# Raw weights of two turns on chip in the first feed-forward product, token sums behind its first turn, and the last operand pair scaled out of place

## The chip, the cores and the metric

The kernel runs on one core of one Trainium2 chip. The metric is the device time of one execution in microseconds, lower is better. Three timed runs of the kernel before give a median of 1869.41 us (1862.83 to 1870.68). The trace shown here is of one profiled execution, which took 1867.55 us.

TensorE multiplies matrices into PSUM banks. VectorE (DVE in the profile), ScalarE (ACT) and GpSimd (POOL) work element by element, and SyncE (SP) issues the DMA transfers. In the program each engine has one fixed order of instructions, so what stands behind a waiting instruction on its engine starts later.

## The reference

One layer of a hybrid decoder over 1024 prompt tokens and 8 sample tokens, in fp32, with a model width of 1024. The change concerns the last two of its steps:

```
x += crossattn(rmsnorm(x), memory K/V)       # 4 heads, 256 memory rows, output product o @ w_xo
x += relu(rmsnorm(x, norm_ffn_g) @ w_up)^2 @ w_down     # 1024 -> 4096 -> 1024
y  = rmsnorm(x, final_g)
rmsnorm(x, g) = x * rsqrt(mean(x * x, -1) + 1e-6) * g
```

## The kernel before

Tokens lie along the free axis (1032 columns, as two halves of HT = 516), features along the partitions. Every fp32 operand of a product is split into a high part (a cast on ACT to fp32r) and a low part (source minus high part, on DVE); `split` (L103 for the cast, L104 for the subtraction) does it, and a product takes three matmuls: high by high, high by low, low by high.

`cross_out` computes the output product of the cross attention, one slice of 128 features at a time (L136), adds the residual x on DVE (L1211), squares the sum on ACT and adds the squares up on POOL into the tile `ssx` (L1217), writes x to DRAM, and scales it in place by `norm_ffn_g` (`scaled`, L1118). The tiles `yq[0..3]` hold two slices each, that is one "pair" of features in four blocks of 516 columns (b11, b12, b21, b22).

The feed-forward part replaces the 8 block products of a 2x2 by 2x2 block product by 7 (a Strassen scheme). `features` builds the seven token-side combinations of each pair by subtraction and splits them into the operands `c_cb0`, `c_cb1` (pairs 0 and 1) and `c_o0`, `c_o1` (pairs 2 and 3). The product then runs in 32 turns: 16 for `w_up` and 16 for `w_down`. In every turn TensorE goes through the 7 steps of `STEPS`: A11, S2, S3, S1, S4, A12, A22, with 24 matmuls of 128x258 each (L1190, tiles `ps_A` and `ps_S`). Four PSUM banks take the products in rotation.

`weights(step, it)` prepares the weights of turn `it` in seven steps: step 0 loads the raw weights, two halves `wr0` (blocks A11 and A21) and `wr1` (A12 and A22), 512 KB each (L1160); steps 1 to 6 form S3, S2, S1 and S4 on POOL (`comb`, L1149) and split each block. `turn` issues, for each step, the matmuls, then `evict`, then `ahead(n)`. `ahead(n)` in turn `it` runs step n of the weights of turn `it+1`, and at n = 6 step 0 of turn `it+2`. All raw weights take their tile from the pool tag `wst`.

In an up turn `up` collects the products in one of the four tiles, `yq[it % 4]`: a copy on ACT for A11 (L1283), additions of PSUM on DVE for the others (L1274), then relu and square on ACT (L1277, L1278). Four results `ht` of further subtractions on POOL (`sub`, L1265) and three blocks of yq go to the DRAM tensor `d_h` (L1261), all issued by SP. From turn 15 on `stage` brings the first combinations of the down turns back from `d_h` into yq tiles (L1380), and the tokens' operands are split from there; later ones come through `fetch` (L1341).

The scale of the norm is applied late: `token_sums` sums the squares per token on TensorE (`ps_ms`, L1242), DVE makes `ms` and its reciprocal (L1248, L1249), and TensorE spreads it over the partitions (`ps_msb`, L1254), from where it is copied over `ssx` (L1256). `residual` multiplies x by it (L1325) and subtracts (L1333) in turns 1 to 12. In the kernel before this stands ahead of the first turn.

Program order is not written out by hand for each engine: a scheduler places the instructions of each engine in the order in which the operands are expected, so a change in the program can also change an engine's order elsewhere.

Of the kernel before, what the change touches and what calls it, by code (L numbers as in the profile page):

```python
# [19 lines left out]
P = 128  # L20
# [3 lines left out]
NB = 8  # L24
# [46 lines left out]
class K:  # L71
# [1036 lines left out]
    def operand(self, pl, tag):  # L1108

        t = pl.tile([P, 2, 7, HT], F32R, tag=tag, name=f"c_{tag}")  # L1110
        return t[:, 0], t[:, 1]

    def scaled(self, i):

        x = self.yq[i]
        for j in range(2):
            xj = x[:, 2 * j:2 * j + 2]
            self.nc.vector.tensor_scalar(xj, xj, self.g["norm_ffn_g"][:, 2 * i + j:2 * i + j + 1], None, op0=ALU.mult)  # L1118

    def features(self, *pairs):  # L1120

        nc = self.nc
        t2 = {i: self.hr.tile([P, HT], F32, tag="hr", name="ft") for i in pairs}
        for c, x, y, z in ((0, 0, None, None), (3, 0, 1, 0), (4, 4, 3, 0), (5, 1, 3, 1), (2, 3, None, None), (1, 2, None, None), (6, 2, 2, 4)):
            for i in pairs:
                blk = [self.yq[i][:, n] for n in range(4)] + [t2[i]]
                if y is not None:
                    (nc.vector if i == 3 and c in (3, 4) else nc.gpsimd).tensor_tensor(blk[x], blk[y], blk[z], op=ALU.subtract)
                if c != 3:
                    self.split(self.b[i][0][:, c], self.b[i][1][:, c], blk[x])  # L1130
            if c == 5:
                for i in pairs:
                    self.split(self.b[i][0][:, 3], self.b[i][1][:, 3], self.yq[i][:, 0])

    def weights(self, step, it):
# [61 lines left out]
    def cross_out(self):  # L1197
        nc, a = self.nc, self.a
        N0 = HALF + NB
        xm = lambda m: self.yq[m // 2][:, 2 * (m % 2):2 * (m % 2) + 2].rearrange("p h t -> p (h t)")  # L1200
        blocks = ((0, N0 // 2), (N0, T), (N0 // 2, N0))
        for ms in ((0, 1), (2,), (3,), (4,), (5,), (6,), (7,)):
# [3 lines left out]
            for m, (b0, b1) in [(m, b) for b in blocks for m in ms]:  # L1206
# [11 lines left out]
            for m in ms:  # L1218
                nc.sync.dma_start(self.d_x[m], xm(m))
            if ms[-1] % 2:  # L1220
                self.scaled(ms[-1] // 2)
            if ms[-1] in (1, 3):
                self.features(ms[-1] // 2)

    def ffn(self, f1):
# [21 lines left out]
        for rr, cc in areas:  # L1247
            nc.vector.tensor_scalar(ms[rr, cc], ps[rr, cc], 1.0 / D, RMS_EPS, op0=ALU.mult, op1=ALU.add)  # L1248
            nc.vector.reciprocal(r2[rr, cc], ms[rr, cc])  # L1249
        for tiles in ((0, 1, 2, 3), (8,), (4, 5, 6, 7)):  # L1250
            ps = bank("ps_msb")[:, 0]
            for j, i in enumerate(tiles):
                n = P if i < 8 else NB
                nc.tensor.matmul(ps[:, j * P:j * P + n], ms[0:n, i:i + 1].broadcast_to([n, P]), self.ident[0:n, 0:n], start=True, stop=True)  # L1254
            c0, n = TC[tiles[0]].start, P * len(tiles) if tiles[0] < 8 else NB
            nc.vector.tensor_copy(self.ssacc[:, c0:c0 + n], ps[:, 0:n])  # L1256
        msb = self.ssacc.rearrange("p (h t) -> p h t", h=2)
# [52 lines left out]
        def down(n, ps):  # L1310
            y = yq[it % 4]
            op = ALU.subtract if n in ("S4", "A22") else ALU.add
# [23 lines left out]
        def sums(j):  # L1336
            nc.sync.dma_start(yq[j].rearrange("p (m h) t -> p m (h t)", m=2), self.d_x[2 * j:2 * j + 2].rearrange("k p t -> p k t"))

# [275 lines left out]
```

## Time and profile before

| | us |
|---|---|
| median of three runs | 1869.41 (1862.83 to 1870.68) |
| profiled execution | 1867.55 |
| span in its trace | 1865.8 |
| TensorE busy | 1677.5 (90%) |
| DVE busy | 1251.6 (67%) |
| POOL busy | 842.5 (45%) |
| ACT busy | 763.1 (41%) |

The span is what the trace covers; the execution is 1.75 us longer. Busy time is summed over the whole span. A stretch of the span is read by its own busy times, and by the granted clock of TensorE beside them, where 1.00 is the higher of its two levels (2.4 GHz) and 0.50 the lower one (1.2 GHz). Feed-forward turns are told apart by the start of their first `ps_S` product, S2, which follows A11.

### The profile page before, as it was taken

How to read it: one execution, taken by the hardware profiler on the slowest of the kernel's cores; microseconds unless marked ns; L12 is line 12 of the kernel's file. 1: busy time of each engine (PE TensorE's matmuls, PEld its weight loads, DVE VectorE, ACT ScalarE, POOL GpSimd, SP SyncE). 2: the span in 40 equal slices, each digit the busy share in tenths (PEclk: the TensorE clock that was granted, in tenths of full speed). 3: DMA queues.
4: the chain of work that ended last, by engine and by line, in shares of the span. 5: the costliest groups of instructions: out<-in, count | busy, mean ns of one | idle time of the engine just before them, and what ended most of it. 6: DMA issues, size and time to landing. Idle time of an engine off the chain costs nothing. (4 is left out here: it accounts for less than half of the span.)

```text
span 1865.8 us, 36912 instructions
## 1 busy us (share of the span) xinstructions
PE 1677.5 (90%) x14667; PEld 1550.3 (83%) x14667; DVE 1251.6 (67%) x2316; ACT 763.1 (41%) x1453; POOL 842.5 (45%) x648
## 2 busy tenths in 40 slices
PE   6988888998995699999999988889998889999997
PEld 5887777887884688878887888889998889999997
DVE  5797687679768855656555456445554498888795
ACT  4535443554532244423332333333333364444442
POOL 6541342134247664654333566674544453322242
PEclk8999777999996899999999998999999999999998
DMA  4313312211223574664443423664444586554542
GB/s 136 112 57 95 111 57 81 66 50 54 68 68 91 147 235 119 213 189 137 149 146 125 148 91 113 185 197 125 126 126 125 171 290 211 153 153 139 148 126 103
DMA packets 248541, 244.20 MB, mean 131 GB/s; under 512 B 24936, under 2 KB 191232, under 8 KB 248368
## 3 DMA queue, kind: packets, MB, share of 16 engines
q1 hardware_dynamic: 248324, 241.82, 42.4%
q8 instruction: 116, 1.90, 0.4%
q14 instruction: 57, 0.47, 0.1%
q10 hardware_dynamic: 44, 0.01, 0.0%
HBM read 179.95 MB, written 61.83 MB: 130 GB/s over the span
## 5 line engine op out<-in xcount | busy, mean ns | idle before, releaser
L1190 PE MATMUL ps_S<-c_cb,wS 128*128 128x258 f32 x1536 | 227.5, 283 | 7.0 <-DVE yq L1315 5.3
L1190 PE MATMUL ps_S<-c_o,wS 128*128 128x258 f32 x1536 | 227.0, 283 | 0.0
L136 PE MATMUL ps_g<-xh,wh 128*128 128x256 f32 (+1 forms) x704 | 216.7, 308 | 11.1 <-DVE raw L369 6.2
L104 POOL TENSOR_TENSOR wl<-wst,wh 128x1024 fp32r<-128x1024 f32 x70 | 169.7, 2424 | 113.1 <-ACT wh L103 99.4
L136 PE MATMUL ps_g<-xl,wh 128*128 128x256 f32 (+1 forms) x704 | 212.2, 302 | 0.8 <-DVE xl L104 0.8
L136 PE MATMUL ps_g<-xh,wl 128*128 128x256 f32 (+1 forms) x704 | 210.7, 299 | 0.1
L1190 PE MATMUL ps_A<-c_cb,wA 128*128 128x258 f32 x1152 | 179.1, 292 | 34.7 <-DVE yq L1274 34.7
L1190 PEld LDWEIGHTS ps_S<-c_cb,wS 128*128 128x128 f32 x1536 | 203.3, 190 | 7.5 <-issue 5.4
L104 DVE TENSOR_TENSOR wS<-rS,wS 128x512 fp32r<-128x512 f32 x96 | 100.4, 1046 | 158.9 <-ACT wS L103 158.9
L1190 PEld LDWEIGHTS ps_S<-c_o,wS 128*128 128x128 f32 x1536 | 202.4, 190 | 0.0
L1190 PEld LDWEIGHTS ps_A<-c_cb,wA 128*128 128x128 f32 x1152 | 158.7, 197 | 37.4 <-issue 36.0
L136 PE MATMUL ps_g<-o,wh 128*128 128x260 f32 (+1 forms) x768 | 176.2, 324 | 7.1 <-DVE yq L1211 3.6
L1190 PE MATMUL ps_A<-c_o,wA 128*128 128x258 f32 x1152 | 177.7, 291 | 0.2 <-DVE c_o L104 0.2
L1149 POOL TENSOR_TENSOR rS<-wr,rS 128x512 f32<-128x512 f32 x64 | 90.6, 1416 | 172.1 <-DMA wr<-in_w_down_dram 82.7
L1190 PEld LDWEIGHTS ps_A<-c_o,wA 128*128 128x128 f32 x1152 | 159.0, 198 | 0.4 <-DVE c_o L104 0.4
L136 PEld LDWEIGHTS ps_g<-xh,wh 128*128 128x128 f32 x704 | 142.8, 203 | 17.1 <-DVE raw L369 6.7
L103 ACT CAST wh<-wst 128x1024 fp32r<-128x1024 f32 x92 | 96.1, 1046 | 135.8 <-PE ps_g L136 67.4
L136 PEld LDWEIGHTS ps_g<-xl,wh 128*128 128x128 f32 x704 | 142.4, 202 | 5.8 <-issue 2.0
L103 ACT CAST wS<-rS 128x512 fp32r<-128x512 f32 x96 | 57.8, 617 | 217.2 <-POOL rS L1149 209.1
L136 PEld LDWEIGHTS ps_g<-o,wh 128*128 128x128 f32 x768 | 128.6, 191 | 20.2 <-issue 6.0
L136 PEld LDWEIGHTS ps_g<-xh,wl 128*128 128x128 f32 x704 | 141.7, 201 | 3.7 <-issue 1.4
L136 PE MATMUL ps_g<-o,wl 128*128 128x260 f32 (+1 forms) x384 | 124.6, 325 | 3.1 <-POOL wl L104 3.1
(481 smaller groups left out, 3891.6 us busy)
## 6 DMA issues: line engine op xcount, KB each, us to landing
hb<-d_h SPq DMA_DIRECT2D x105, 258.0 KB
wst<-in_w_in_dram SPq DMA_DIRECT2D x44, 512.0 KB
d_h<-ht SPq DMA_DIRECT2D x64, 258.0 KB
wr<-in_w_up_dram SPq DMA_DIRECT2D x32, 512.0 KB
wr<-in_w_down_dram SPq DMA_DIRECT2D x26, 512.0 KB
d_h<-yq SPq DMA_DIRECT2D x48, 258.0 KB
wst<-in_w_out_dram SPq DMA_DIRECT2D x16, 512.0 KB
ck<-in_cache_mem_k_dram SPq DMA_DIRECT2D x32, 256.0 KB
```

What stands on the lines that cost most here:

```text
L103: (heng or nc.scalar.copy)(hi, src)
L104: (eng or nc.vector).tensor_tensor(lo, src, hi.bitcast(F32), op=ALU.subtract)
L136: nc.tensor.matmul(ps, l[:, k, :], r[:, cols], start=(k == 0 and i == 0), stop=(k == kt - 1 and i == 2))
L1149: nc.gpsimd.tensor_tensor(R[n], R[x], R[y], op=op)
L1190: nc.tensor.matmul(ps[:, s], l[:, i, :], r[:, c, cols], start=k == 0 and j == 0, stop=k == 3 and j == 2)
```

## The change

The edits, in the order of the program:

- In `cross_out` raw x lies in the yq tiles 2, 3, 0, 1 instead of 0, 1, 2, 3. Pair 3, raw in `yq[1]`, is scaled out of place into `yq[3]`, block of columns by block (a new `tensor_scalar` on DVE), instead of in place in two instructions.
- The token-side subtractions are put into `first_diff` and `second_diffs`, called as soon as a pair is scaled; `features` then mostly splits. The order of the splits is 0, 4, 5, 3, 2, 1, 6.
- The token sums and their spreading (`mean_squares`) move from before turn 0 into `ahead(6)` of turn 0; `residual` moves by one turn, to turns 2 to 13.
- The raw weights of odd up turns are loaded into `yq[2]`, those of even turns into the `wst` tiles. Step 0 for turn `it+2` is called at n = 0 of turn `it` (for `it` under 15) instead of n = 6.
- The up turns collect their products in two tiles, `yq[(it + 1) % 2]`, instead of four.
- The first three stage loads move: the first to the end of turn 13, the second to the start of turn 15 (before, both were in turn 14); the stage tiles and the tiles of the down turns' sums are numbered anew to fit.

The core of the diff:

```
+    def first_diff(self, i):
+        b11, b12, b21, b22 = self.blocks(i)
+        t1 = self.hr.tile([P, HT], F32, tag="hr", name="t1")
+        self.nc.gpsimd.tensor_tensor(t1, b12, b11, op=ALU.subtract)
+        self.td[i] = [t1]
+
+    def second_diffs(self, i):
+        b11, b12, b21, b22 = self.blocks(i)
+        t2 = self.hr.tile([P, HT], F32, tag="hr", name="t2")
+        eng = self.nc.vector if i == 3 else self.nc.gpsimd
+        eng.tensor_tensor(t2, b22, self.td[i][0], op=ALU.subtract)
+        eng.tensor_tensor(b12, b22, b12, op=ALU.subtract)
+        self.td[i].append(t2)
...
+        for c in (0, 4, 5, 3, 2, 1, 6):
             for i in pairs:
-                blk = [self.yq[i][:, n] for n in range(4)] + [t2[i]]
-                if y is not None:
-                    (nc.vector if i == 3 and c in (3, 4) else nc.gpsimd).tensor_tensor(blk[x], blk[y], blk[z], op=ALU.subtract)
-                if c != 3:
-                    self.split(self.b[i][0][:, c], self.b[i][1][:, c], blk[x])
-            if c == 5:
-                for i in pairs:
-                    self.split(self.b[i][0][:, 3], self.b[i][1][:, 3], self.yq[i][:, 0])
+                b11, b12, b21, b22 = self.blocks(i)
+                t1, t2 = self.td[i]
+                if c == 6:
+                    self.nc.gpsimd.tensor_tensor(b21, b21, t2, op=ALU.subtract)
+                src = {0: b11, 4: t2, 5: b12, 3: t1, 2: b22, 1: b21, 6: b21}[c]
+                self.split(self.b[i][0][:, c], self.b[i][1][:, c], src)
...
-                t = self.wp.tile([P, 4, 256], F32, tag="wst", name=f"wr{r}")
+                if it < 16 and it % 2:
+                    t = self.yq[2].rearrange("p b t -> p (b t)")[:, r * 1024:(r + 1) * 1024].rearrange("p (i m) -> p i m", i=4)
+                else:
+                    t = self.wp.tile([P, 4, 256], F32, tag="wst", name=f"wr{r}")
...
+        raw = [self.yq[i] for i in (2, 3, 0, 1)]
+        self.xs = raw[0:3] + [raw[1]]
+        self.td = {}
+        xm = lambda m: raw[m // 2][:, 2 * (m % 2):2 * (m % 2) + 2].rearrange("p h t -> p (h t)")
...
+                if m >= 6:
+                    xg = self.xs[3][:, 2 * (m - 6):2 * (m - 6) + 2].rearrange("p h t -> p (h t)")[:, b0:b1]
+                    nc.vector.tensor_scalar(xg, x, self.g["norm_ffn_g"][:, m:m + 1], None, op0=ALU.mult)
...
-            if ms[-1] % 2:
-                self.scaled(ms[-1] // 2)
-            if ms[-1] in (1, 3):
-                self.features(ms[-1] // 2)
+            i = ms[-1] // 2
+            if ms[-1] in (1, 3, 5):
+                self.scaled(i)
+                self.first_diff(i)
+                self.second_diffs(i)
+                if i < 2:
+                    self.features(i)
+            elif ms[-1] == 6:
+                self.first_diff(3)
+            elif ms[-1] == 7:
+                self.second_diffs(3)
...
-        ps = token_sums("ps_ms")
...
+        def mean_squares():
+
+            ps = token_sums("ps_ms")
...
-            y = yq[it % 4]
+            y = yq[(it + 1) % 2]
...
-            if n == 6 and it < 30:
+            if (n == 6 or it < 15 and n == 0) and it < 30 and it + 2 not in self.w:
                 self.weights(0, it + 2)
             c = self.STEPS[n][1]
-            if 1 <= it <= 12 and n == 1:
-                residual((it - 1) // 3, (it - 1) % 3)
-            if it == 14 and n in (1, 4):
-                stage(n // 4)
+            if it == 0 and n == 6:
+                mean_squares()
+            if 2 <= it <= 13 and n == 1:
+                residual((it - 2) // 3, (it - 2) % 3)
+            if it == 13 and n == 6:
+                stage(0)
             if it == 15:
+                if n == 0:
+                    stage(1)
                 if n == 2:
                     stage(2)
                 for i, b in enumerate(self.b):
                     self.split(b[0][:, c], b[1][:, c], staged[n][:, i])
-                if n in (0, 1, 2, 4):
-                    stage({0: 3, 1: 4, 2: 5, 4: 6}[n])
+                if n in (0, 1, 3, 4):
...
-            x = yq[(0, 1, 2, 0, 1, 2, 1)[n]]
+            x = yq[(3, 2, 1, 3, 2, 3, 2)[n]]
...
+        acc = [yq[i] for i in (1, 3, 2, 0)]
```

In the rows below a name with a number is one tile instance. On TensorE, at the passage from the last product of the cross attention (`ps_g`, L136) to turn 0, the kernel before has:

```order
L136 MATMUL ps_g_12520<-o0_9361,wh_12457 128x260 x2
L136 MATMUL ps_g_12520<-o0_9361,wl_12458 128x260
L1242 MATMUL ps_ms_12636<-ones_487,ssx_11742 128x1 x8
L1242 MATMUL ps_ms_12636<-ones_487,ssx_11742 8x1
L1254 MATMUL ps_msb_12652<-ident_116,ms_12646 128x128 x4
L1254 MATMUL ps_msb_12658<-ident_116,ms_12646 128x8
L1254 MATMUL ps_msb_12661<-ident_116,ms_12646 128x128 x4
L1190 MATMUL ps_A11_12667<-c_cb0_11747,wA11_12569 128x258 x3
L1190 MATMUL ps_A11_12667<-c_cb1_11748,wA11_12569 128x258 x3
L1190 MATMUL ps_A11_12667<-c_o0_12553,wA11_12569 128x258 x3
```

and the changed kernel (`ps_A11`, `ps_S2` and so on are the products of the steps; its matmuls are L1206):

```order
L136 MATMUL ps_g_12534<-o0_9361,wh_12469 128x260 x2
L136 MATMUL ps_g_12534<-o0_9361,wl_12470 128x260
L1206 MATMUL ps_A11_12644<-c_cb0_11747,wA11_12585 128x258 x3
L1206 MATMUL ps_A11_12644<-c_cb1_11748,wA11_12585 128x258 x3
L1206 MATMUL ps_S2_12674<-c_cb0_11747,wS2_12591 128x258 x3
L1206 MATMUL ps_S2_12674<-c_cb1_11748,wS2_12591 128x258 x3
L1206 MATMUL ps_S3_12708<-c_cb0_11747,wS3_12595 128x258 x3
L1206 MATMUL ps_S3_12708<-c_cb1_11748,wS3_12595 128x258 x3
L1206 MATMUL ps_S1_12737<-c_cb0_11747,wS1_12598 128x258 x3
L1206 MATMUL ps_S1_12737<-c_cb1_11748,wS1_12598 128x258 x3
L1206 MATMUL ps_A11_12644<-c_o0_12569,wA11_12585 128x258
L1206 MATMUL ps_S2_12674<-c_o0_12569,wS2_12591 128x258
```

The sums and their spreading are gone from between the two, and the parts of A11, S2, S3 and S1 that need only `c_cb` stand ahead of the first that need `c_o`. In the changed kernel the sums stand on TensorE between the last step of turn 0 and the first of turn 1:

```order
L1206 MATMUL ps_A22_12843<-c_o0_12569,wA22_12607 128x258 x3
L1206 MATMUL ps_A22_12843<-c_o1_12570,wA22_12607 128x258 x3
L1272 MATMUL ps_ms_12877<-ones_487,ssx_11742 128x1 x8
L1272 MATMUL ps_ms_12877<-ones_487,ssx_11742 8x1
L1286 MATMUL ps_msb_12891<-ident_116,ms_12642 128x128 x4
L1286 MATMUL ps_msb_12897<-ident_116,ms_12642 128x8
L1286 MATMUL ps_msb_12900<-ident_116,ms_12642 128x128 x4
L1206 MATMUL ps_A11_12910<-c_cb0_11747,wA11_12702 128x258 x3
L1206 MATMUL ps_A11_12910<-c_cb1_11748,wA11_12702 128x258 x3
```

They now lie behind the whole of turn 0. On POOL, around the results `ht` of turn 7 (collected in `yq3` before), the kernel before has, with `wr*_14604` the raw weights of turn 9:

```order
L1265 TENSOR_TENSOR ht_14526<-yq3_11746 128x516
L1149 TENSOR_TENSOR rS3_14664<-wr0_14604 128x512
L1265 TENSOR_TENSOR ht_14561<-yq3_11746 128x516
L1265 TENSOR_TENSOR ht_14564<-yq3_11746,ht_14561 128x516
L1265 TENSOR_TENSOR ht_14609<-yq3_11746,ht_14564 128x516
L1149 TENSOR_TENSOR rS2_14669<-wr1_14606,rS3_14664 128x512
L1149 TENSOR_TENSOR wr0_14604<-wr0_14604,wr1_14606 128x4x128
L1149 TENSOR_TENSOR rS2_14669<-wr1_14606,rS2_14669 128x512
```

and the changed kernel (turn 7 collects in `yq0`; `yq2` holds the raw weights of turn 9, `wr*_14627` those of turn 10, and the operation of L1149 is L1162):

```order
L1297 TENSOR_TENSOR ht_14519<-yq0_11743 128x516
L1162 TENSOR_TENSOR rS2_14662<-yq2_11745,rS3_14657 128x512
L1297 TENSOR_TENSOR ht_14554<-yq0_11743 128x516
L1297 TENSOR_TENSOR ht_14557<-yq0_11743,ht_14554 128x516
L1297 TENSOR_TENSOR ht_14598<-yq0_11743,ht_14557 128x516
L1162 TENSOR_TENSOR rS2_14662<-yq2_11745,rS2_14662 128x512
L1162 TENSOR_TENSOR rS3_14901<-wr0_14627 128x512
L1162 TENSOR_TENSOR wr0_14627<-wr0_14627,wr1_14629 128x4x128
```

S2 of turn 9 moved ahead of three of the `ht`, and S3 and S1 of turn 9 are no longer in this stretch; in their place stand S3 and S1 of turn 10. On SP, in the same stretch, the kernel before has:

```order
L1261 DMA d_h_70<-yq3_11746 128x516
L1160 DMA wr0_14604<-in_w_up_dram 128x4x256
L1261 DMA d_h_70<-ht_14526 128x516
L1261 DMA d_h_70<-yq3_11746 128x516
L1261 DMA d_h_70<-ht_14561 128x516
L1261 DMA d_h_70<-yq3_11746 128x516
L1261 DMA d_h_70<-ht_14564 128x516
L1160 DMA wr1_14606<-in_w_up_dram 128x4x256
L1261 DMA d_h_70<-ht_14609 128x516
```

and the changed kernel:

```order
L1176 DMA wr0_14627<-in_w_up_dram 128x4x256
L1293 DMA d_h_70<-ht_14519 128x516
L1293 DMA d_h_70<-yq0_11743 128x516
L1293 DMA d_h_70<-ht_14554 128x516
L1293 DMA d_h_70<-yq0_11743 128x516
L1293 DMA d_h_70<-ht_14557 128x516
L1293 DMA d_h_70<-ht_14598 128x516
L1176 DMA wr1_14629<-in_w_up_dram 128x4x256
L1293 DMA d_h_70<-yq1_11744 128x516
```

The place of the two loads among the stores is much the same; before, they bring the weights of turn 9, now those of turn 10.

## Rows read from the trace of the kernel before

**Rows 1.** The page: busy time, its share of the span, and instructions, by engine.

```profile
PE 1677.5 (90%) x14667; PEld 1550.3 (83%) x14667; DVE 1251.6 (67%) x2316; ACT 763.1 (41%) x1453; POOL 842.5 (45%) x648
```

**Rows 2.** Windows by stage: length, PE, PEld, DVE, ACT, POOL busy, clock, DMA share, GB/s.

```profile
1110.00:1130.00 20.00, 7.62 (x48) 7.01 (x47) 17.78 (x17) 9.68 (x17) 14.57 (x9) 0.69 0.25 79
1157.90:1489.90 332.00, 298.47 (x2355) 295.96 (x2354) 164.13 (x196) 125.19 (x223) 178.86 (x131) 0.95 0.50 153
1489.90:1541.00 51.10, 42.78 (x339) 41.82 (x338) 47.08 (x64) 33.33 (x61) 24.09 (x11) 0.97 0.85 290
1541.00:1561.20 20.20, 20.20 (x171) 20.20 (x170) 20.20 (x26) 8.01 (x13) 11.96 (x8) 1.00 0.62 184
```

**Rows 3.** Critical chain in the down turns: start, us, what.

```profile
1541.14 11.50 PE ps_S L1190 x96
1552.64 8.63 PE ps_A L1190 x72
1561.27 11.48 PE ps_S L1190 x96
```

**Rows 4.** Waits in the up turns, 1160 to 1500: engine and line, releaser, total, times, longest.

```profile
ACT wS L103 <- POOL rS L1149: 146.5, 14, 12.2
...
POOL rS L1149 <- DMA wr<-in_w_up_dram: 85.3, 24, 6.3
...
PE ps_A L1190 <- DVE yq L1274: 33.5, 14, 4.0
```

**Rows 5.** Critical chain around turns 7 to 9.

```profile
1324.12 1.29 POOL ht L1265
...
1333.59 4.92 DMA wr<-in_w_up_dram
1338.58 1.32 POOL rS L1149
...
1340.57 1.11 DVE wS L104
1341.68 0.60 DVE yq L1274
1342.29 1.31 DVE wS L104
1343.60 0.62 DVE yq L1274
...
1351.50 0.49 ACT yq L1283
```

**Rows 6.** Groups of the up turns on DVE, 1160 to 1500, each shape apart.

```profile
L104 DVE TENSOR_TENSOR wS<-rS,wS 128x512 fp32r<-128x512 f32 x42 | 53.5, 1274 | 132.6 <-ACT wS L103 132.6
L1274 DVE TENSOR_TENSOR yq<-ps_S,yq 128x516 f32<-128x516 f32 x71 | 47.4, 683 | 3.8 <-PE ps_S L1190 3.7
```

**Rows 7.** Timeline of 1112 to 1142 on TensorE.

```profile
1120.01 2.84 PE L1242 MATMUL ps_ms<-ones,ssx 128*128 128x1 f32 x14 [4.62 <-POOL ssx L1217]
1130.74 4.36 PE L1254 MATMUL ps_msb<-ident,ms 128*128 128x128 f32 x18 [7.89 <-DVE ms L1248]
1134.86 0.96 PE L1190 MATMUL ps_A<-c_cb,wA 128*128 128x258 f32 x6
```

**Rows 8.** Timeline of the same stretch on DVE.

```profile
1114.24 0.43 DVE L1211 TENSOR_TENSOR yq<-ps_g,yq 128x260 f32<-128x260 f32 x1 [0.77 <-PE ps_g L136]
...
1115.19 0.69 DVE L104 TENSOR_TENSOR wS<-wr,wS 128x512 fp32r<-128x512 f32 x1
...
1122.13 5.12 DVE L104 TENSOR_TENSOR c_o<-yq,c_o 128x516 fp32r<-128x516 f32 x3
```

**Rows 9.** Timeline of 1157 to 1159.5 on TensorE.

```profile
1157.90 0.89 PE L1190 MATMUL ps_S<-c_cb,wS 128*128 128x258 f32 x6
```

**Rows 10.** Critical chain from turn 15 on.

```profile
1498.87 4.50 DMA d_h<-ht
1503.38 8.30 DMA hb<-d_h
```

More of the change, by code (lines that the diff above doesn't have):

```diff
@@ L1111, in operand, with blocks @@
         return t[:, 0], t[:, 1]
+    def blocks(self, i):
+        return [self.xs[i][:, n] for n in range(4)]
     def scaled(self, i):
-        x = self.yq[i]
+        x = self.xs[i]
         for j in range(2):
@@ L1118, in scaled @@
             self.nc.vector.tensor_scalar(xj, xj, self.g["norm_ffn_g"][:, 2 * i + j:2 * i + j + 1], None, op0=ALU.mult)
+    def first_diff(self, i):
[10 more added lines that the diff above has]
+        self.td[i].append(t2)
     def features(self, *pairs):
-        nc = self.nc
-        t2 = {i: self.hr.tile([P, HT], F32, tag="hr", name="ft") for i in pairs}
-        for c, x, y, z in ((0, 0, None, None), (3, 0, 1, 0), (4, 4, 3, 0), (5, 1, 3, 1), (2, 3, None, None), (1, 2, None, None), (6, 2, 2, 4)):
+        for c in (0, 4, 5, 3, 2, 1, 6):
             for i in pairs:
-                blk = [self.yq[i][:, n] for n in range(4)] + [t2[i]]
-                if y is not None:
-                    (nc.vector if i == 3 and c in (3, 4) else nc.gpsimd).tensor_tensor(blk[x], blk[y], blk[z], op=ALU.subtract)
-                if c != 3:
-                    self.split(self.b[i][0][:, c], self.b[i][1][:, c], blk[x])
-            if c == 5:
-                for i in pairs:
-                    self.split(self.b[i][0][:, 3], self.b[i][1][:, 3], self.yq[i][:, 0])
+                b11, b12, b21, b22 = self.blocks(i)
[4 more added lines that the diff above has]
+                self.split(self.b[i][0][:, c], self.b[i][1][:, c], src)
     def weights(self, step, it):
@@ L1199, in cross_out @@
         N0 = HALF + NB
-        xm = lambda m: self.yq[m // 2][:, 2 * (m % 2):2 * (m % 2) + 2].rearrange("p h t -> p (h t)")
+        raw = [self.yq[i] for i in (2, 3, 0, 1)]
+        self.xs = raw[0:3] + [raw[1]]
+        self.td = {}
+        xm = lambda m: raw[m // 2][:, 2 * (m % 2):2 * (m % 2) + 2].rearrange("p h t -> p (h t)")
         blocks = ((0, N0 // 2), (N0, T), (N0 // 2, N0))
@@ L1243, in token_sums @@
             return ps
-        ps = token_sums("ps_ms")
         ms, r2 = f1.tile([P, 9], F32, name="ms"), f1.tile([P, 9], F32, name="r2")
[L1247 to L1256, printed above, removed]
+        def mean_squares():
+            ps = token_sums("ps_ms")
+            for rr, cc in areas:
+                nc.vector.tensor_scalar(ms[rr, cc], ps[rr, cc], 1.0 / D, RMS_EPS, op0=ALU.mult, op1=ALU.add)
+                nc.vector.reciprocal(r2[rr, cc], ms[rr, cc])
+            for tiles in ((0, 1, 2, 3), (8,), (4, 5, 6, 7)):
+                ps = bank("ps_msb")[:, 0]
+                for j, i in enumerate(tiles):
+                    n = P if i < 8 else NB
+                    nc.tensor.matmul(ps[:, j * P:j * P + n], ms[0:n, i:i + 1].broadcast_to([n, P]), self.ident[0:n, 0:n], start=True, stop=True)
+                c0, n = TC[tiles[0]].start, P * len(tiles) if tiles[0] < 8 else NB
+                nc.vector.tensor_copy(self.ssacc[:, c0:c0 + n], ps[:, 0:n])
         msb = self.ssacc.rearrange("p (h t) -> p h t", h=2)
@@ L1310, in down @@
         def down(n, ps):
-            y = yq[it % 4]
+            y = acc[it % 4]
             op = ALU.subtract if n in ("S4", "A22") else ALU.add
@@ L1336, in sums @@
         def sums(j):
-            nc.sync.dma_start(yq[j].rearrange("p (m h) t -> p m (h t)", m=2), self.d_x[2 * j:2 * j + 2].rearrange("k p t -> p k t"))
+            nc.sync.dma_start(acc[j].rearrange("p (m h) t -> p m (h t)", m=2), self.d_x[2 * j:2 * j + 2].rearrange("k p t -> p k t"))
         def fetch(pair, n):
@@ L1358, in ahead @@
                     self.split(b[0][:, c], b[1][:, c], staged[n][:, i])
-                if n in (0, 1, 2, 4):
-                    stage({0: 3, 1: 4, 2: 5, 4: 6}[n])
+                if n in (0, 1, 3, 4):
+                    stage({0: 3, 1: 4, 3: 5, 4: 6}[n])
                 if n == 3:
@@ L1363, in ahead @@
             if t == 1 and n == 0:
-                y = yq[3]
+                y = yq[0]
                 sub(5, y[:, 3], y[:, 1])
@@ L1389, in ffn @@
             if t >= 12:
-                y = yq[t - 12]
+                y = acc[t - 12]
                 for k in (2, 1):
@@ L1416, in ffn @@
         nc.sync.dma_start(gfin, a["final_g"].unsqueeze(0).broadcast_to([P, D]))
-        yt = lambda j, m: yq[j].rearrange("p (m h) t -> p m (h t)", m=2)[:, m]
+        yt = lambda j, m: acc[j].rearrange("p (m h) t -> p m (h t)", m=2)[:, m]
         n = 0
```

## Prediction

> **What bounds the kernel now.** I read the page first, then windows by stage, then the waits and the chain inside the stage that stood out. The page shows TensorE busy for 1677.5 us of the span [rows 1], so 188 us at most are idle, and the question is where. The windows answer that: in a down turn TensorE is busy without a break at a clock of 1.00, while in the up turns it is busy for 298.47 of 332 us at 0.95, at the passage from up to down for 42.78 of 51.1, and ahead of turn 0 for 7.62 of 20 [rows 2]. The change touches just these three stretches.
>
> A turn that nothing holds up lasts 1561.27 - 1541.14 = 20.13 us: 96 matmuls of S in 11.5 and 72 of A in 8.63 [rows 3]. From S2 of turn 1 to S2 of turn 15 are 14 turns in 332.0 us, where 14 x 20.13 = 281.8 would do, so the up turns lose 50.2 us. Of these TensorE waits 33.5 us, once in each turn, for a DVE eviction of PSUM [rows 4]; the other 17 agree with a clock of 0.95 instead of 1.00 over 332 us [rows 2].
>
> DVE was not short of time: it is busy 164.13/14 = 11.7 us per up turn, POOL 12.8 and ACT 8.9 [rows 2]. The chain tells why the eviction is late [rows 5]. The load of the second half of the raw weights of turn 9 goes out at 1333.59, behind the stores of turn 7, and takes 4.92 us. POOL forms S2 at 1338.58, ACT casts it, DVE splits it at 1340.57, and only behind this split stands the next eviction, at 1341.68; then again a split and an eviction. TensorE stands meanwhile, its banks full. The largest waits of the stretch are links of this one chain: POOL for the weights' DMA, 85.3 us, and ACT for POOL, 146.5 us [rows 4].
>
> **The change, part by part.** *Raw weights of two turns on chip.* The order shows the two loads of the stretch at the same places between the stores of turn 7, but they now bring turn 10 and not turn 9. The halves of turn 9 have landed a turn, some 20 us, before S2 is formed, so the 4.92 us of the DMA and its place in SP's queue leave the chain. S2 of turn 9 stands on POOL directly behind the first `ht` of turn 7, which was at 1324.12, and not behind all four; it would be formed near 1325.4 and split some 3 us later, near 1328.4, where before the split ended at 1341.68 [rows 5]. DVE then waits for products of TensorE, which is how it should be. What is late next is S4 of turn 9, which stands behind the last `ht`: that ends near 1334.5 by three of some 1.4 us, S4 is split near 1337.5, and its split's place on DVE is behind the eviction of A12 of turn 8, near 1325.7 + 11.5 + 2.9 = 1340. So some 2.5 us of slack at the tightest place, and the loads of POOL and DVE leave 7 us per turn. S3 and S1 of the turn after come behind and have most of a turn. I take a period of 20.3 us: 14 x 20.3 = 284.2, a gain of 48. Bounds: 50.2, all of it, and 42, 0.6 us left in each turn.
>
> The two output tiles in place of four add a wait: ACT's copy of A11 of turn 9 must find the stores of turn 7 done. In the chain before, that copy is at 1351.50 [rows 5], some 17 us behind the last of these stores; with two stalls less it comes some 7 us sooner. A store takes 4.50 us [rows 10]. Some 5 us remain, and I cost this at nothing; without that cover each us too late is 14 us in all, and ACT's casts of weights queue behind it.
>
> *Sums behind turn 0, features, last pair out of place.* Before, TensorE does 14 of the 18 sums at 1120.01, the spreading at 1130.74 to 1135.1, and A11 only at 1134.86 [rows 7], although the last gemm's eviction is at 1114.24 [rows 8]. Turn 1's S2 begins at 1157.90 [rows 9]. In the new order TensorE begins turn 0 right behind the gemm, with 24 matmuls that need only pairs 0 and 1, and goes on as splits of pairs 2 and 3 come. From 1114.7 DVE has 19 instructions up to the last of these splits. One takes 0.69 us at 1115.19 and 1.71 at 1122.13 [rows 8]: 13 or 32 us. I take 1.2, between the two, since fewer POOL subtractions lie beside: 23 us, the last split at 1137.5, and A22, which needs it, ends 2.9 later. With TensorE at the lower clock for part of that, as it had 0.69 on average in 1110 to 1130 [rows 2], I put turn 0's end at 1142. Now the sums are on the path: 2.84/14 x 18 = 3.65, then 4.36 for the spreading, 8.0 in the slow stretch of before [rows 7], half of it at the full clock; I take 6. DVE stands at `ms` meanwhile with one split of weights behind, which is hidden. Then A11, 8.63/3 = 2.9, and S2 of turn 1 at 1151: 7 us gained. Bounds: with 13 us of DVE TensorE is the limit, from the first split near 1118 with 144 matmuls at 0.12 us, 1135.5, then 4.1 and 2.9: 1142.5, a gain of 15. With 32 us: 1147 + 2.9 + 8.0 + 2.9 = 1161, a loss of 3. The residual one turn later moves nothing in sum, since POOL has room; its two loads and stores per turn go with it on SP.
>
> *The passage.* From S2 of turn 15 to the down turns are 51.1 us in place of 40.3. DVE is busy for 47.08 of them and the DMA engines for 0.85 at 290 GB/s [rows 2]; the splits and loads that make it so all stay. Only one stage load of 1.06 MB comes before turn 15 now, not two. If transfers decide, that costs 1.06 MB / 290 GB/s = 3.6 us; if DVE does, nothing. The chain there runs through a load of 8.30 us [rows 10]. The weights come early in turn 15 too, which may give back up to 5. I take a loss of 1, bounds -3.6 and +5.
>
> The sum, against the profiled execution's 1867.55 us: -48 - 7 + 1 = -54, so 1813.5, rounded to 1813. The median of the runs is 1.9 us above that execution, well inside the range.
>
> **The rivals.** *The chain stays, only shorter (0.14).* POOL, ACT and DVE each work in order, and if S2 or S4 still comes behind an `ht` that waits for ACT, an eviction is late in each turn, with a fall of the clock behind it. For it: S4's small slack. Against it: four banks cover one late eviction. Half of the 50.2 would stay: 1867.55 - 25 - 7 + 1 = 1836.5.
>
> *The start is bound by DVE at the loaded price (0.12).* Every split beside POOL takes 1.71 us, and the start loses 3: 1867.55 - 48 + 3 + 1 = 1823.5. For it: three splits in a row did so [rows 8]. Against it: six subtractions of POOL are earlier now.
> The Trainium skill, "SBUF — State Buffer", section "Who interferes with whom", has a rule that speaks for this rival: a DVE instruction with two inputs in SBUF and a GpSimd instruction that reads SBUF exclude each other for the whole instruction. The trace agrees, with 0.69 and 1.71 us for the same shape. By that rule the splits in the up turns, 1.27 us in the mean against 0.68 for an eviction from PSUM [rows 6], would get no cheaper either, which the up turns' idle time covers.
>
> *Two output tiles are too few (0.04).* The copy of A11 waits for a store that lands late, behind a load on SP, in every up turn. It decides from 5 us of extra delay on, and at 4 us per turn beyond that all the gain is gone. With one more transfer of 4.92 us [rows 5] in series a turn is 25.05 us, 350.7 for 14: 1867.55 + 18.7 - 7 + 1 = 1880, slower than before. Against it: in the new order no store of turn 7 stands behind the load that waits.
>
> *The change doesn't do what it says (0.03).* The loads come early and something else in the chain, not seen, has the same length: the start's gain alone, 1861, no measurable change.
>
> **How the numbers follow.** The forecast, up turns bound by TensorE, has 0.67: 1813, with bounds 1867.55 - 50.2 - 15 - 5 = 1797 and 1867.55 - 42 + 3 + 3.6 = 1832. With the first rival the range is 1797 to 1837. I count 0.5% (9.3 us) as the least that a measurement tells from no change. Faster has the forecast and the first two rivals, 0.93; same 0.03; slower 0.04.
>
> **What would show it.** In the profile after, S2 of two up turns should begin 20.1 to 20.4 us apart, the wait of TensorE's `ps_A` for the DVE eviction should be gone, POOL should wait for the weights' DMA no more, and the clock over the up turns should be 1.00. Turn 1's S2 should begin near 1151, behind the sums. The passage should still take about 51 us with DVE nearly full. I am wrong if a wait of TensorE for an eviction is left in each turn, with S4's or S2's split ahead of it, or if ACT's copy waits for the DMA of a store.

## The result and the profile after

The changed kernel takes 1811.18 us (median of four runs, 1807.32 to 1817.54) against 1866.12 for the kernel before beside it: a ratio of 0.9709, 95% interval 0.9668 to 0.9749, faster. The forecast was 1813 us in a range of 1797 to 1837. Its profiled execution took 1810.41 us with a span of 1808.7, 57.1 less than before.

The windows of the changed kernel, by the same stages as [rows 2]; the columns are length, PE, PEld, DVE, ACT and POOL busy, granted clock, DMA share and GB/s. The rows are the 20 us behind the last matmul of the cross attention's output, the 14 turns from S2 of turn 1 to S2 of turn 15, the passage from there to S2 of turn 18, and a down turn. The passage is taken to S2 of turn 18 and not of turn 17, since the changed kernel begins turn 17 inside the last steps of turn 16; before, the same stretch took 51.10 + 20.20 = 71.3 us [rows 2].

```profile
1119.30:1139.30 20.00, 17.85 (x148) 17.66 (x148) 16.11 (x26) 11.34 (x22) 14.57 (x7) 1.00 0.35 106
1153.70:1435.20 281.50, 281.50 (x2354) 281.50 (x2353) 157.31 (x197) 134.27 (x226) 188.79 (x133) 1.00 0.56 175
1435.20:1503.30 68.10, 62.99 (x506) 62.12 (x505) 61.96 (x90) 39.77 (x72) 22.49 (x15) 0.97 0.89 294
1503.30:1523.40 20.10, 20.10 (x170) 20.10 (x169) 16.08 (x25) 8.66 (x15) 6.77 (x5) 1.00 0.57 179
```

In the up turns TensorE is busy for the whole 281.5 us at a clock of 1.00, where it was 298.47 of 332 us at 0.95 [rows 2]. DVE, ACT and POOL have nearly the same busy time as before, in a shorter stretch. The passage is still the place where DVE (61.96 of 68.1) and DMA (0.89) are nearly full. The chain of the changed kernel shows the up turns as the chain of before showed the down turns [rows 3], TensorE alone:

```profile
1153.88 11.47 PE ps_S L1206 x96
1165.35 8.62 PE ps_A L1206 x72
1173.97 11.51 PE ps_S L1206 x96
1185.48 8.62 PE ps_A L1206 x72
```

The waits of the same stretch (engine and line, releaser, total, times, longest) answer to [rows 4]. DVE now waits for TensorE's products, and POOL for DVE's splits, which free the tiles that its results go to. The waits of POOL for the DMA of weights have shrunk from 85.3 us to the two lines shown, 7.0 us in three waits. No wait of TensorE matmuls is in the list, and none of ACT's copy of A11 for a DMA.

```profile
POOL rS L1162 <- DVE wS L104: 50.5, 21, 5.9
...
DVE yq L1306 <- PE ps_S L1206: 49.8, 46, 1.6
...
ACT wS L103 <- POOL rS L1162: 26.3, 6, 7.1
...
POOL yq L1162 <- DMA yq<-in_w_up_dram: 3.5, 1, 3.5
POOL wr L1162 <- DMA wr<-in_w_up_dram: 3.5, 2, 2.8
```

At the start, the timeline of TensorE (start, us, instruction; in brackets the idle time before it and what ended it) answers to [rows 7, 9]. A11 begins right behind the product, the sums are behind turn 0, and A11 of turn 1 at 1149.62:

```profile
1119.93 0.96 PE L1206 MATMUL ps_A<-c_cb,wA 128*128 128x258 f32 x6 [0.61 <-ACT wS L103]
...
1136.05 0.98 PE L1206 MATMUL ps_A<-c_cb,wA 128*128 128x258 f32 x6 [1.54 <-DVE yq L1306]
...
1141.90 1.96 PE L1272 MATMUL ps_ms<-ones,ssx 128*128 128x1 f32 x18
1145.37 4.60 PE L1286 MATMUL ps_msb<-ident,ms 128*128 128x128 f32 x18 [1.51 <-DVE ms L1280]
1149.62 1.64 PE L1206 MATMUL ps_A<-c_cb,wA 128*128 128x258 f32 x6
...
1153.72 0.89 PE L1206 MATMUL ps_S<-c_cb,wS 128*128 128x258 f32 x6
```

Where the time went, each stretch in us by the starts of its first matmuls, in this profile and in those of the experiments:

| kernel | up to the cross attention's output product | that product, first to last matmul | to S2 of turn 1 | 14 turns, to S2 of turn 15 | to S2 of turn 31 | the rest | us, median |
|---|---|---|---|---|---|---|---|
| before | 1001.6 | 112.3 | 44.0 | 332.0 | 333.0 | 43.0 | 1866.12 |
| changed | 995.7 | 123.3 | 34.7 | 281.5 | 329.8 | 43.6 | 1811.18 |
| changed, once more | 997.0 | 121.7 | 33.1 | 288.6 | 329.1 | 44.2 | 1816.98 |
| e1, one store of weights | 993.7 | 115.5 | 35.0 | 326.7 | 331.9 | 42.2 | 1857.18 |
| e1, late call | 999.6 | 119.8 | 34.4 | 281.8 | 329.4 | 43.6 | 1810.32 |
| e2, sums first | 996.5 | 119.2 | 42.2 | 282.6 | 329.1 | 43.8 | 1819.13 |
| e3, tile places | 1000.3 | 116.9 | 33.2 | 282.4 | 329.7 | 44.7 | 1810.17 |
| e4, load held | 997.9 | 115.4 | 35.7 | 282.9 | 328.5 | 43.2 | 1813.38 |
| e5, both | 998.8 | 112.2 | 34.4 | 283.1 | 326.8 | 42.5 | 1799.69 |
| e6, sums split | 1001.0 | 121.0 | 27.7 | 284.5 | 330.2 | 43.4 | 1810.90 |
| e7, all three | 995.4 | 111.8 | 28.6 | 284.1 | 330.7 | 44.5 | 1802.25 |
| e8, in place | 996.4 | 120.0 | 34.7 | 282.7 | 328.6 | 43.6 | 1809.69 |

The first column is the part that the diff does not touch. Its 12 values lie between 993.7 and 1001.6 and the one of before is the highest, so the 5.9 us that the changed kernel seems to gain there are scatter. The second column is a surprise: the product ahead of the feed-forward part became 11.0 us longer, and again 9.4 longer in the second profile of the changed kernel.

The timelines show two differences that can be the cause; e3 to e5 below test them. The first: on SP, the two loads of the raw weights of turn 1 into `yq2` (L1176) go out at 1057.06, ahead of the store of a slice of x (L1242), and on DVE the scaling in place (L1121) waits 7.50 us for that store, 3.96 before the change. From the issue of the store to the scaling it is 1067.66 - 1059.58 = 8.1 us, and 1063.48 - 1058.95 = 4.5 before. The next eviction stands behind it, and the one after that waits 5.29 us for a TensorE that has itself been held up. TensorE's granted clock over the product is 0.93, where it was 0.98 before the change and is 0.98 again in e5 below. The rows of the changed kernel, on SP and on DVE:

```profile
1019.53 3.81 SPq L1225 DMA_DIRECT2D yq<-d_x  x8
...
1057.06 2.42 SPq L1176 DMA_DIRECT2D yq<-in_w_up_dram  x2
1059.58 0.46 SPq L1242 DMA_DIRECT2D d_x<-yq  x1
```

```profile
1067.66 0.76 DVE L1121 TENSOR_SCALAR yq<-yq,prm 128x1032 f32<-128x1032 f32 x1 [7.50 <-DMA d_x<-yq]
...
1071.07 1.02 DVE L1231 TENSOR_TENSOR yq<-ps_g,yq 128x512 f32<-128x512 f32 x2
1077.38 0.43 DVE L1231 TENSOR_TENSOR yq<-ps_g,yq 128x260 f32<-128x260 f32 x1 [5.29 <-PE ps_g L136]
```

The rows of the kernel before that answer to them:

```profile
1004.80 23.53 SPq L1205 DMA_DIRECT2D yq<-d_x  x8
...
1058.95 0.34 SPq L1219 DMA_DIRECT2D d_x<-yq  x1
```

```profile
1063.48 0.76 DVE L1118 TENSOR_SCALAR yq<-yq,prm 128x1032 f32<-128x1032 f32 x1 [3.96 <-DMA d_x<-yq]
```

The first row on SP is the second difference: the eight loads of raw x go out from 1019.53 on, where before the first of them went out at 1004.80. In the changed kernel raw x of the first slices lies in `yq2`, another place in memory; that this place is freed later is what e3 tests.

### The profile page after: what moved, and what is told of

Same layout as the page of the kernel before. It is cut to its first block, busy times and chain, and to the rows that moved or that the text cites. A ratio compares the mean times of both kernels' runs of the same rounds, so it can differ in the third digit from the quotient of the medians.

```text
span 1808.7 us, 36951 instructions
## 1 busy us (share of the span) xinstructions
PE 1664.0 (92%) x14667; PEld 1539.1 (85%) x14667; DVE 1233.4 (68%) x2320; ACT 772.2 (43%) x1453; POOL 844.7 (47%) x648
## 3 DMA queue, kind: packets, MB, share of 16 engines
q1 hardware_dynamic: 248324, 241.82, 43.6%
## 5 line engine op out<-in xcount | busy, mean ns | idle before, releaser
L136 PE MATMUL ps_g<-xh,wh 128*128 128x256 f32 (+1 forms) x704 | 216.4, 308 | 11.1 <-DVE raw L369 6.2
L1206 PE MATMUL ps_S<-c_o,wS 128*128 128x258 f32 x1536 | 226.4, 282 | 0.0
L1206 PE MATMUL ps_S<-c_cb,wS 128*128 128x258 f32 x1536 | 226.0, 282 | 0.0
L136 PE MATMUL ps_g<-xl,wh 128*128 128x256 f32 (+1 forms) x704 | 211.9, 301 | 0.5 <-DVE xl L104 0.5
L136 PE MATMUL ps_g<-xh,wl 128*128 128x256 f32 (+1 forms) x704 | 210.4, 299 | 0.1
L1206 PEld LDWEIGHTS ps_S<-c_cb,wS 128*128 128x128 f32 x1536 | 201.9, 189 | 0.0
L1206 PEld LDWEIGHTS ps_S<-c_o,wS 128*128 128x128 f32 x1536 | 201.8, 189 | 0.0
L136 PE MATMUL ps_g<-o,wh 128*128 128x260 f32 (+1 forms) x768 | 179.0, 327 | 13.2 <-DVE yq L1231 9.8
L1206 PE MATMUL ps_A<-c_cb,wA 128*128 128x258 f32 x1152 | 172.6, 284 | 7.3 <-ACT c_cb L103 5.1
L1206 PE MATMUL ps_A<-c_o,wA 128*128 128x258 f32 x1152 | 173.2, 284 | 0.0
L1206 PEld LDWEIGHTS ps_A<-c_cb,wA 128*128 128x128 f32 x1152 | 153.2, 190 | 8.1 <-ACT c_cb L103 5.5
L136 PEld LDWEIGHTS ps_g<-xh,wh 128*128 128x128 f32 x704 | 142.7, 203 | 17.1 <-DVE raw L369 6.7
L1206 PEld LDWEIGHTS ps_A<-c_o,wA 128*128 128x128 f32 x1152 | 153.7, 191 | 0.4 <-DVE c_o L104 0.4
L136 PEld LDWEIGHTS ps_g<-o,wh 128*128 128x128 f32 x768 | 130.7, 194 | 26.4 <-issue 9.5
L136 PEld LDWEIGHTS ps_g<-xl,wh 128*128 128x128 f32 x704 | 142.2, 202 | 5.5 <-issue 2.0
L136 PEld LDWEIGHTS ps_g<-xh,wl 128*128 128x128 f32 x704 | 141.5, 201 | 3.7 <-issue 1.4
L1162 POOL TENSOR_TENSOR rS<-wr,rS 128x512 f32<-128x512 f32 x48 | 70.5, 1468 | 127.8 <-DMA wr<-in_w_down_dram 63.9
L136 PE MATMUL ps_g<-o,wl 128*128 128x260 f32 (+1 forms) x384 | 125.5, 327 | 1.4 <-POOL wl L104 1.4
L104 DVE TENSOR_TENSOR wS<-rS,wS 128x512 fp32r<-128x512 f32 x96 | 81.5, 849 | 36.9 <-ACT wS L103 36.7
```

The costliest lines, as they stand in the source:

```text
L104: (eng or nc.vector).tensor_tensor(lo, src, hi.bitcast(F32), op=ALU.subtract)
L136: nc.tensor.matmul(ps, l[:, k, :], r[:, cols], start=(k == 0 and i == 0), stop=(k == kt - 1 and i == 2))
L1162: nc.gpsimd.tensor_tensor(R[n], R[x], R[y], op=op)
L1206: nc.tensor.matmul(ps[:, s], l[:, i, :], r[:, c, cols], start=k == 0 and j == 0, stop=k == 3 and j == 2)
```

## Experiments

**One store for the raw weights** undoes the part that the forecast rested on most, and keeps the rest.

```diff
-                if it < 16 and it % 2:
+                if False:
-            if (n == 6 or it < 15 and n == 0) and it < 30 and it + 2 not in self.w:
+            if n == 6 and it < 30:
```

> The changed kernel with the raw weights of all up turns in the wst tiles again and their load called at n = 6; two output tiles, sums behind turn 0 and the new cross_out stay. Theory (the late raw weights made the stalls of the up turns): the period of an up turn goes back from 20.11 us to about 23.7, S2 of turn 1 to S2 of turn 15 takes 325 to 335 us in place of 281.5, and the time is 1855 to 1865. Rival (the other edits, such as the features' order or the sums' place, removed the stalls): the period stays at 20.1 and the time near 1811. Rival (two output tiles have a price of their own, hidden while weights are early): the period goes above 24 us, with ACT's copy of A11 waiting for a store's DMA, and the time above 1870.

The time was 1857.18 us, ratio 0.9954 (0.9927 to 0.998). The 14 turns took 326.7 us, and the waits in 1170 to 1470 are those of before again:

```profile
ACT wS L103 <- POOL rS L1162: 131.6, 13, 11.9
...
POOL rS L1162 <- DMA wr<-in_w_up_dram: 69.6, 21, 4.6
...
PE ps_A L1206 <- DVE yq L1306: 29.4, 11, 5.1
```

So the late raw weights made the stalls, with 45 us of 50. The two output tiles cost nothing that shows: no wait of ACT's copy of A11 for a DMA is in this kernel's list of waits either. That the 14 turns were not longer than before says less, since the first two of them took 20.1 us each, where before they took 25.1 and 23.8, and the other twelve took 286.5 us against 283.1. What this kernel keeps of the other edits is 0.5%.

**The call alone.** The load called at n = 6 again, weights of odd turns still in `yq2`:

```diff
-            if (n == 6 or it < 15 and n == 0) and it < 30 and it + 2 not in self.w:
+            if n == 6 and it < 30:
```

> The changed kernel with the load of the raw weights called at n = 6 of turn it again, but odd turns still in yq2. Theory (it is the free tile that lets the load go early, since the scheduler places a load by when its tile is free): up turns stay at 20.1 us and the time is 1805 to 1817. Rival (the earlier call is what brings the weights early): up turns of 22 us and more, 1838 or above.

A single run gave 1810.32 us and 281.8 us for the 14 turns. The free tile is what matters; the earlier call does nothing more that shows.

**Sums ahead of turn 0.**

```diff
+        mean_squares()
         msb = self.ssacc.rearrange("p (h t) -> p h t", h=2)
...
-            if it == 0 and n == 6:
-                mean_squares()
```

> The changed kernel with the token sums and their spreading ahead of turn 0 again. Theory (the sums' place is what the start gains from): from the last matmul of the cross attention's output to S2 of turn 1 it takes some 43 us, as before the change, and not 34.5; the time is 1817 to 1822. Rival (the new order of the features and of their subtractions is what gains): that stretch takes 36 to 38 us and the time is about 1813.

The time was 1819.13 us (ratio 0.9742, 0.97 to 0.9783), and the stretch to S2 of turn 1 took 42.2 us, as the first theory says: of the 9.3 us won there the sums' place is worth 42.2 - 34.7 = 7.5. The rest, 1.8 us, may be the new order of the features, but is not shown: the kernels with the sums behind turn 0 and their spreading unchanged spread from 33.1 to 35.7 in this stretch. The time by itself, in the range of the theory, is not told from the changed kernel's. TensorE idles 10 us for the last sum of squares:

```profile
1116.63 0.58 PE L1272 MATMUL ps_ms<-ones,ssx 128*128 128x1 f32 x4 [0.61 <-DVE yq L1231]
1127.21 2.84 PE L1272 MATMUL ps_ms<-ones,ssx 128*128 128x1 f32 x14 [10.00 <-POOL ssx L1240]
1130.38 4.60 PE L1286 MATMUL ps_msb<-ident,ms 128*128 128x128 f32 x18 [0.33 <-DVE ms L1280]
```

**Places of the tiles, and the load of turn 1 held back**, first apart, then together.

```diff
-            self.yq = [yq.tile([P, 4, HT], F32, name=f"yq{i}") for i in range(4)]
+            tl = [yq.tile([P, 4, HT], F32, name=f"yq{i}") for i in (2, 3, 0, 1)]
+            self.yq = [tl[i] for i in (2, 3, 0, 1)]
```

> The changed kernel with the four yq tiles laid out in memory in the order 2, 3, 0, 1, so that the slices of x needed first in the cross attention's output lie where they lay before the change. Theory (the first loads of x wait for a piece of memory that the cross attention's sample part gives free later): the first load of x is issued some 15 us earlier on SP, near 1004 in place of 1019.5, and TensorE gets back the some 5.5 us that it lost on its way through the first two slices of that product; time 1804 to 1807. Rival (the loss there is of another cause, as the run's own spread upstream): no change, 1811.

```diff
                 if i < 2:
                     self.features(i)
+                else:
+                    for k in (0, 2):
+                        nc.gpsimd.tensor_tensor(self.yq[2][:, k, 0:1], self.xs[2][:, k, 0:1], self.xs[2][:, k + 1, 0:1], op=ALU.subtract)
```

> The changed kernel with two tiny POOL subtractions (128x1 each) into yq2 behind the scaling of pair 2, so that the raw weights of turn 1 can be loaded only after them and stand on SP behind the stores of slices 2 to 5 of x. Theory (these two loads of 512 KB, ahead of the store of slice 2, make the store late, the scaling of pair 1 wait 7.5 us in place of 4.0, and the evictions behind it on DVE hold up TensorE): that wait is 4 us again, TensorE's idle time there falls by some 4 to 5 us, and the time is 1805 to 1808. Rival (the wait is the store's own latency): no change, 1811, or slower by 1 to 3 us where the later load holds up turn 1.

The times, 1810.17 us (ratio 0.9704, 0.9635 to 0.9773) and 1813.38 (0.9721, 0.9661 to 0.978), are not the expected ones and don't tell either from the changed kernel. The stretches do: 116.9 and 115.4 us for the product, where the six profiles that keep both places have 119.2 to 123.3. In e3 the first load of x went out at 1003.50, as expected; in e4 the longest wait for the store of x fell from 7.5 us to 4.4. The first experiment's kernel, which has no load into `yq2`, agrees with e4: 115.5 us.

> The changed kernel with the tile places of before for the raw x and the load of turn 1's weights held back until pair 2 is scaled: the edits of e3 and e4 together. Theory (the two losses in the cross attention's output are separate and are the change's): the stretch from its first to its last matmul is near 112 us, as before, no long wait for the store of x is left, and the time is 1802 to 1806. Rival (what is won there is lost again by a later start of turn 1 or is within the spread of the runs): 1809 to 1813.

Together the product took 112.2 us, as before the change, and the time was 1799.69 us, below the expected range: ratio 0.9644 (0.9611 to 0.9678), against 0.9722 (0.9684 to 0.9759) for the changed kernel in the same comparison. The two losses are the change's and separate. By e3 and e4 the load costs 116.9 - 112.2 = 4.7 us and the places of the tiles 3.2; that is 7.9 together, within the 6.9 to 11.0 us by which the six profiles with both are longer than before. Of the 16.0 us between the two profiled executions of this comparison, 9.5 are the product and 5.5 the up turns, where the changed kernel had one long turn (see below). On DVE the wait for the store of x is back at 3.93:

```profile
1061.82 0.76 DVE L1122 TENSOR_SCALAR yq<-yq,prm 128x1032 f32<-128x1032 f32 x1 [3.93 <-DMA d_x<-yq]
...
1065.26 1.03 DVE L1232 TENSOR_TENSOR yq<-ps_g,yq 128x512 f32<-128x512 f32 x2
1069.25 0.43 DVE L1232 TENSOR_TENSOR yq<-ps_g,yq 128x260 f32<-128x260 f32 x1 [2.96 <-PE ps_g L136]
```

> The changed kernel once more, unaltered, timed beside the next three. Every theory expects about 1811 us and a ratio to the kernel before of 0.971; its profile tells how far the stretch of the cross attention's output, 123.3 us from its first matmul to its last in the first profile, differs between two executions. If most of the 11 us that this stretch lost against before is chance, it is nearer to 115 here; if it is the change's, 118 to 124.

The changed kernel once more gave 1816.98 us, with 121.7 us for the product: the loss is the change's.

**The spreading three products later.**

```diff
+
+        def spread():
             for tiles in ((0, 1, 2, 3), (8,), (4, 5, 6, 7)):
...
             if it == 0 and n == 6:
                 mean_squares()
+            if it == 1 and n == 2:
+                spread()
```

> The changed kernel with the token sums behind turn 0 as they are, but their spreading over the partitions only at step 2 of turn 1, three products later. Theory (TensorE's wait for DVE's ms and the lower clock behind it cost part of the break between the turns): the break between the last matmul of turn 0 and the first of turn 1 falls from 7.7 us to about 2, the spreading takes 2 to 3 us in place of 4.6 at the full clock, and the time is 1806 to 1809. Rival (the spreading costs the same wherever it stands): 1811.

The spreading took 2.45 us and waited for nothing, where it took 4.60 behind a wait of 1.51, at a granted clock of 0.50. The break between the turns was 1.90 us, as expected:

```profile
1144.94 1.97 PE L1272 MATMUL ps_ms<-ones,ssx 128*128 128x1 f32 x18
1146.84 0.98 PE L1206 MATMUL ps_A<-c_cb,wA 128*128 128x258 f32 x6
...
1155.54 2.45 PE L1288 MATMUL ps_msb<-ident,ms 128*128 128x128 f32 x18
```

From the product's last matmul to S2 of turn 2 it took 27.7 + 22.4 = 50.1 us, in place of 34.7 + 20.1 = 54.8 and 53.2. The time, 1810.90 us (0.9707, 0.9674 to 0.974), is above the expected 1806 to 1809 and not told from the changed kernel's: the gain is read from the stretch alone.

> The edits of e5 and e6 together on the changed kernel. Theory (the three losses add up): 1797 to 1802 us, ratio to the kernel before 0.964 to 0.968. Rival (only the break between the turns is real): 1806 to 1809.

All three gave 1802.25 us (0.966, 0.9621 to 0.97): faster than the kernel before; the interval just overlaps that of the changed kernel (0.9684 to 0.9759). It is not told from e5, which has the better median, so the times do not show that the third part adds to the other two. The shortest span of all, 1795.0 us, is this kernel's.

**Pair 3 in place.** The diff shown here leaves out that the scaling block by block goes out, and that `yq1` and `yq3` change places in the up turns, the stages and the sums.

```diff
-        self.xs = raw[0:3] + [raw[1]]
+        self.xs = raw
...
+            if ms[-1] >= 6:
+                m = ms[-1]
+                xg = self.xs[3][:, 2 * (m - 6):2 * (m - 6) + 2]
+                nc.vector.tensor_scalar(xg, xg, self.g["norm_ffn_g"][:, m:m + 1], None, op0=ALU.mult)
```

> The changed kernel with pair 3 scaled in place again, slice by slice, each time behind the store of its raw slice, and turn 0's products in yq3 in place of yq1 so that nothing else waits (the two tiles change places in the stages and sums as well). Theory (the scaling out of place spares the wait for the store of the last slice): from the last matmul of the cross attention's output to S2 of turn 1 it takes 36 to 39 us in place of 33 to 35, and the time is 1813 to 1817. Rival (the store is landed before DVE comes to the scaling, since it splits the other pair meanwhile): no change, 34 us and 1811 to 1815, as the changed kernel's own two medians.

The time was 1809.69 us (0.9693, 0.9652 to 0.9733) and the stretch to S2 of turn 1 took 34.7 us: the rival was right. DVE comes to the last scaling at 1123.80, six splits of the other pair later, and does not wait:

```profile
1116.75 0.43 DVE L1231 TENSOR_TENSOR yq<-ps_g,yq 128x260 f32<-128x260 f32 x1 [0.90 <-PE ps_g L136]
...
1122.59 1.29 DVE L104 TENSOR_TENSOR c_o<-yq,c_o 128x516 fp32r<-128x516 f32 x2
1123.80 0.75 DVE L1250 TENSOR_SCALAR yq<-yq,prm 128x1032 f32<-128x1032 f32 x1
```

So of the change's parts this one is worth nothing that can be seen.

## Why the prediction was right, and where it was not

*What bounds the kernel.* Right. The late load of raw weights, POOL's S2, the split and the eviction behind it were the chain of the up turns; with one store for the weights it came back.

*Up turns.* Forecast 48 us, measured 332.0 - 281.5 = 50.5, at the bound. The period is 20.11 us and not 20.3. The slack at S4, put at 2.5 us behind the last `ht`, was larger from turn 9 on: S4 of turn 10 waits 5.84 us for DVE's split of S2, whose tile it takes, ends at 1323.32 and is split only at 1329.85.

```profile
1322.03 1.29 POOL L1162 TENSOR_TENSOR rS<-wr,rS 128x512 f32<-128x512 f32 x1 [5.84 <-DVE wS L104]
```

```profile
1329.85 0.70 DVE L104 TENSOR_TENSOR wS<-rS,wS 128x512 fp32r<-128x512 f32 x1
```

It is thin in turns 5 and 6, up to which the scheduler has put all of POOL's work for `residual`. In the second profile of the changed kernel turn 5 took 27.2 us: POOL waited 9.15 us for a load of the residual, S4 stood behind it, and TensorE waited 4.66 us for an eviction. This is the first rival's chain, in a single turn and started by another load:

```profile
1237.84 1.27 POOL L1357 TENSOR_TENSOR xv<-xv,ssx 128x516 f32<-128x516 f32 x1 [9.15 <-DMA xv<-d_x]
1239.07 1.26 POOL L1162 TENSOR_TENSOR rS<-yq,rS 128x512 f32<-128x512 f32 x1
```

```profile
1242.86 1.63 PE L1206 MATMUL ps_S<-c_cb,wS 128*128 128x258 f32 x6 [4.66 <-DVE yq L1306]
```

It is not a matter of that profile alone. The eight other profiles with weights in `yq2`, all but the first of the changed kernel, have turn 5 or 6 longer by 0.3 to 1.6 us in all, and in each POOL waits 5.8 to 8.1 us at the residual in turn 5. The prediction had put the residual at nothing, since POOL has room; it is the waits for its loads that the up turns have little room for.

*Two output tiles at nothing.* Right: the copy of A11 waits for no store, with early weights or with late ones.

*The start.* Forecast 7, measured 44.0 - 34.7 = 9.3 from the end of the product on. The terms were off both ways. Most of DVE's splits took 0.69 us and not 1.2, and TensorE, not DVE, set the pace: turn 0 took it 21.97 us, 20.43 of them busy at a clock of 1.00. So turn 0 ended 22.6 us behind the product's last eviction, 1141.90 - 1119.35, and not 28; the break of the sums took 1149.62 - 1141.90 = 7.7 us and not 6, and A11 of turn 1 behind it, at a granted clock of 0.69, 4.1 and not 2.9.

*The product of the cross attention.* Here a step failed. The change was costed only from the last eviction on; the renumbered tiles and the new load's place on SP were taken as free, and cost 11.0 us in the profile, 6.9 to 11.0 over the six profiles that keep both. That load was in the order of SP, between the loads of `w_xo` and a store of x that DVE waits for. The sum came out right since other terms made up for it: 2.5 in the up turns, 2.3 at the start, 4.2 in the passage, and 5.9 of scatter upstream. That these cancel to 3 us is luck; that the up turns carry the gain is not.

*The passage.* Forecast a loss of 1, measured a gain of 333.0 - 329.8 = 3.2 up to S2 of turn 31. Turn 15 took 20.1 us in place of 23.3, and 23.7 with late weights, so the gain is that of the early weights, which the bound of +5 had allowed for; the whole stretch says it less clearly, with 331.9 for late weights and 326.8 to 330.7 in the other profiles. The stage load moved into turn 15 did not lengthen that turn.

*The rivals.* The chain did not stay in each turn; what is left of it is in turns 5 and 6, small but for one profile. The start was not bound by DVE at the loaded price. Output tiles were not too few, and the change did what it says.

## What to carry over

A buffer more, so that a load can go out a whole turn earlier, can be worth the full stall where a DMA stands in a loop with three engines in order: here 45 of 50 us. But look at where that load, its first instance above all, now stands on its queue, and at who gives the memory of every renumbered tile free: here two such places cost some 7 to 11 us, beside the 57 won. A difference between two profiles is compared stretch by stretch, the untouched ones too, before it is put down to the change.

## What was not expected of the hardware

At the start one POOL subtraction of 128x512, 1.3 us elsewhere, took 7.73 us while DVE did a row of 11 splits without a pause, at 0.69 us each; it ended 1.2 us behind the last of them. It took 7.73 or 7.74 us in seven other profiles at the same place.

```profile
1122.67 7.73 POOL L1162 TENSOR_TENSOR rS<-yq,rS 128x512 f32<-128x512 f32 x1 [2.68 <-DVE wS L104]
1130.37 0.74 POOL L1240 TENSOR_TENSOR ssx<-ssx,xsq 128x260 f32<-128x260 f32 x1
1131.07 2.55 POOL L1144 TENSOR_TENSOR yq<-yq,t 128x516 f32<-128x516 f32 x2
```

```profile
1122.50 0.69 DVE L104 TENSOR_TENSOR c_o<-yq,c_o 128x516 fp32r<-128x516 f32 x1
...
1124.93 2.50 DVE L104 TENSOR_TENSOR c_o<-yq,c_o 128x516 fp32r<-128x516 f32 x4
1127.36 0.69 DVE L104 TENSOR_TENSOR c_o<-t,c_o 128x516 fp32r<-128x516 f32 x1
...
1133.05 1.13 DVE L104 TENSOR_TENSOR c_o<-yq,c_o 128x516 fp32r<-128x516 f32 x1 [3.80 <-ACT c_o L103]
```

The forecast had reckoned with the opposite, DVE slowed beside POOL, at 1.2 us a split and in its rival at 1.71 [rows 8]. Both agree with the rule cited there from the Trainium skill, "SBUF — State Buffer", section "Who interferes with whom": whichever of the two starts first has the port for its whole instruction, and the other waits. By these rows a row of DVE instructions can keep POOL out for all its length. It need not: in e8 DVE's row had no pause either, and POOL's subtraction came in between two splits, took 1.62 us, and it was DVE's split that took longer, 1.80.

```profile
1118.73 1.62 POOL L1162 TENSOR_TENSOR rS<-yq,rS 128x512 f32<-128x512 f32 x1 [1.73 <-DVE wS L104]
```

```profile
1119.10 1.80 DVE L104 TENSOR_TENSOR c_o<-t,c_o 128x516 fp32r<-128x516 f32 x1
```

What decides which of the two goes next is not shown. The long subtraction was not free: the last subtraction of the features stood behind it on POOL, and DVE's last splits waited 3.80 us.
